# First MLP product turned token-major, two of its eight K pairs by a seven-product scheme, h kept in DRAM

## The chip, the cores and the metric

The kernel runs on one core of a Trainium2 chip. The metric is the device time of one execution in microseconds (us); the figure of a kernel is the median of several runs.

## The reference, cut to what matters

One layer of a hybrid block: 256 tokens, model width D = 2048, MLP width 8192, all in fp32. The part that the change touches is the end of it:

```
n = rms_norm(h);  h = h + concat(y_A, y_B) @ W_out          # mixers, out projection 2048 x 2048
h = h + square(relu(rms_norm(h) @ W1)) @ W2                  # W1 2048 x 8192, W2 8192 x 2048
out = rms_norm(h)
```

The row factor of the second `rms_norm` is taken out of the MLP: relu squared passes a positive row factor r on as r*r, and the kernel multiplies by it (`fs`) at the very end.

## The kernel before, in words

**How fp32 products are made.** TensorE multiplies in fp32r, a reduced fp32. So each operand is split into a rounded part hi and a remainder lo: ScalarE casts hi (`split`, L117) and VectorE subtracts lo = w - hi (L118). A product is the sum of three: hi*hi, hi*lo and lo*hi. A weight tile `w` of 128x2048 (1 MB) comes by one DMA of the SP queue into one of three buffers and is split in two pieces of 1024 columns. The split pairs have three buffers.

**Stages.** In projection and the two mixers (to 500 us of the span), out projection (L659, two halves `nh` of 1024 output columns, 508 to 555), first MLP product, here FF1 (L704 and L705, 555 to 919), second MLP product, here FF2 (L721, from 919), and the tail with the last norm.

**Out projection.** Each half accumulates four PSUM banks `accs`. VectorE adds each to the residual (L664) into `h`, which stays in SBUF to the end. ScalarE squares `h` for the norm (L666). TensorE transposes 128x128 blocks of `h` into the four banks `accb` (L673), and `to_T` writes them out, scaled by the norm's weight, as `hT`: ScalarE the hi part (L162), VectorE the lo part (L163). In `hT` each K block has 256 columns of hi and 256 of lo.

**FF1.** Output columns in 16 groups of four blocks of 128. The weight block is the stationary operand (128x128) and the activations move: L704 moves 512 columns (hi and lo of `hT` against hi of w) and L705 moves 256 (hi of `hT` against lo of w). The result stands feature-major, which is how FF2 wants its stationary operand. A group ends with four copies on ScalarE (L708) and on VectorE four additions (L709) and four relu-times-itself (L710), each 128x256, into `g`.

**FF2.** 64 K blocks `f`. `gs`, the split of a block of `g`, is stationary; the weights move in 512 columns; eight banks accumulate token-major.

**Pools and order.** PSUM has eight banks: pool `psA` (`acc`) has four, `psB` (`accb`) four. A scheduler in the framework sets one static order per engine from the program's text, and each engine carries out its own order, so an instruction that waits holds up all behind it on that engine.

Of the kernel before, what the change touches and what calls it, by code (L numbers as in the profile page):

```python
# [25 lines left out]
NM = NL + 1  # L26

_CONST_COLS = {}


def _constants():
# [42 lines left out]
def hybrid_block(ctx: ExitStack, tc: tile.TileContext, x, xt, w_in, w_ab, params, w_out, w_ff1, w_ff2,  # L74
# [14 lines left out]
    psA = ctx.enter_context(tc.tile_pool(name="psA", bufs=4, space=PSUM))  # L89

    yctx = ExitStack()
    ypool = yctx.enter_context(tc.tile_pool(name="ypool", bufs=1))
    NYA = 12
    yTa = ypool.tile([P, NYA, 2 * T], F32R, tag="yT", name="yTa")
# [7 lines left out]
    def acc_a():  # L102
        return psA.tile([P, 512], F32, tag="acc", name="acc")
# [19 lines left out]
        return hi, lo  # L123


    big = bpool.tile([P, 2 * D], F32, tag="h", name="big")
    x3 = big.rearrange("p (k t) -> p k t", k=KT)
    cst = cpool.tile([P, consts.shape[1]], F32, tag="cst", name="cst")
# [8 lines left out]
    SP.dma_start(cst, consts)  # L137
    wab = mp.tile([P, KT, 16], F32, tag="Xt", name="wab")
    SP.dma_start(wab, w_ab)

    def C(name):
        a, b = _CONST_COLS[name]
        return cst[:, a:b]

    ident, ones = C("ident"), C("ones")
    eps = C("eps")
# [14 lines left out]
    def to_T(dst, k, pt, wcol):  # L161
        ACT.activation(dst[:, k, 0:T], pt, AF.Copy, scale=wcol)  # L162
        DVE.scalar_tensor_tensor(out=dst[:, k, T:2 * T], in0=pt, scalar=wcol,  # L163
                                 in1=dst[:, k, 0:T].bitcast(F32), op0=ALU.mult, op1=ALU.subtract)
# [466 lines left out]
    mctx.close()  # L631


    psB = ctx.enter_context(tc.tile_pool(name="psB", bufs=4, space=PSUM))
# [5 lines left out]
    h = bpool.tile([P, 2 * D], F32, tag="h", name="h").rearrange("p (f c) -> p f c", f=2)  # L640
    for hf in range(2):
        SP.dma_start(h[:, hf, :], x[hf * P:(hf + 1) * P, :])
    octx = ExitStack()
    op = octx.enter_context(tc.tile_pool(name="op", bufs=1))
    sqj = op.tile([P, 1024], F32, tag="sqj", name="sqj")
    fs = cpool.tile([P, 16], F32, tag="fs", name="fs")
    for nh in range(2):
        accs = [acc_a() for _ in range(4)]
        for kp in range(8):
            w = wtile()  # L650
            SP.dma_start(w, w_out[nh * 8 + kp])
            for kk in range(2):
                k = 2 * kp + kk
                hi, lo = split(w[:, kk * 1024:(kk + 1) * 1024], 1024)
                for hf in range(2):
                    for a, ww in ((0, hi), (T, hi), (0, lo)):
                        st = yT(k, a + hf * P, a + hf * P + P)
                        for c in range(2):
                            PE.matmul(accs[2 * hf + c], lhsT=st, rhs=ww[:, c * 512:(c + 1) * 512],  # L659
                                      start=(k == 0 and a == 0 and ww is hi), stop=(k == 2 * NH - 1 and ww is lo))  # L660
        for hf in range(2):
            for c in range(2):
                hv = h[:, hf, nh * 1024 + c * 512:nh * 1024 + (c + 1) * 512]
                DVE.tensor_tensor(out=hv, in0=accs[2 * hf + c], in1=hv, op=ALU.add)  # L664
            hv = h[:, hf, nh * 1024:(nh + 1) * 1024]
            ACT.activation(sqj, hv, AF.Square, accum_out=fs[:, 2 * hf + nh:2 * hf + nh + 1])  # L666
        for k2 in range(4):
            pt = acc_b()
            for kk in range(2):
                k = nh * 8 + k2 * 2 + kk  # L670
                ptk = pt[:, kk * T:(kk + 1) * T]
                for hf in range(2):
                    PE.transpose(ptk[:, hf * P:(hf + 1) * P], h[:, hf, k * P:(k + 1) * P], ident)  # L673
                to_T(hT, k, ptk, cols[:, 16 + k:17 + k])
# [14 lines left out]
    def g(f):  # L689
        return gt[f // NG][:, f % NG, :]  # L690

    nfw = fp.tile([P, D], F32, tag="nfw", name="nfw")
    for fg in range(NF // 4):
        accs = [acc_a() if fg % 2 == 0 else acc_b() for _ in range(4)]
        for kq in range(4):
            w = wtile()
            SP.dma_start(w, w_ff1[fg * 4 + kq])
            for q in range(2):
                hi, lo = split(w[:, q * 1024:(q + 1) * 1024], 1024)
                for kk in range(2):  # L700
                    k = 4 * kq + 2 * q + kk
                    for f in range(4):
                        cs = slice(kk * 512 + f * P, kk * 512 + (f + 1) * P)
                        PE.matmul(accs[f], lhsT=hi[:, cs], rhs=hT[:, k, :], start=(k == 0), stop=False)  # L704
                        PE.matmul(accs[f][:, T:], lhsT=lo[:, cs], rhs=hT[:, k, 0:T], start=False, stop=(k == KT - 1))  # L705
        for f in range(4):
            lot = fp.tile([P, T], F32, tag="lotf", name="lotf", bufs=2)
            ACT.copy(lot, accs[f][:, T:])  # L708
            DVE.tensor_tensor(out=lot, in0=accs[f][:, 0:T], in1=lot, op=ALU.add)  # L709
            DVE.scalar_tensor_tensor(out=g(4 * fg + f), in0=lot, scalar=0.0, in1=lot, op0=ALU.max, op1=ALU.mult)  # L710
    SP.dma_start(nfw, norm_final_w.unsqueeze(0).to_broadcast([P, D]))

    accs = [[acc_a() for _ in range(4)], [acc_b() for _ in range(4)]]
    TAIL = 3
    held = []

    def ff2(f, hf, c, gs, hl):
        hi, lo = hl[c // 2]
        cs = slice((c % 2) * 512, (c % 2 + 1) * 512)
        for a, ww in ((0, hi), (T, hi), (0, lo)):  # L720
            PE.matmul(accs[hf][c], lhsT=gs[:, a + hf * P:a + hf * P + P], rhs=ww[:, cs],  # L721
                      start=(f == 0 and a == 0 and ww is hi), stop=(f == NF - 1 and ww is lo))

    keep = None
    for f in range(NF):
        w = wtile()
        SP.dma_start(w, w_ff2[f])
        gs = fp.tile([P, 2 * T], F32R, tag="gs", name="gs", bufs=4)
        split(g(f), None, gs[:, 0:T], gs[:, T:])
        n = f - (NF - TAIL)  # L730
        if n == 0:
            keep = fp.tile([P, TAIL - 1, 2, D], F32R, tag="g0", name="keep")
        hl = []
        for q in range(2):
            qs = slice(q * 1024, (q + 1) * 1024)
            if 0 <= n < TAIL - 1:
                hl.append(split(w[:, qs], None, keep[:, n, 0, qs], keep[:, n, 1, qs]))
            else:
                hl.append(split(w[:, qs], 1024))
        if n >= 0:  # L740
            held.append((f, gs, hl))
            continue
        for q in range(2):
            for hf in range(2):
                for c in (2 * q, 2 * q + 1):
                    ff2(f, hf, c, gs, hl)
    fin = fp.tile([P, 12], F32, tag="fin", name="fin")
    sqf = fp.tile([P, 512], F32, tag="sqf", name="sqf")
    o = fp.tile([P, D], F32, tag="o", name="o", bufs=1)
    NP = 5  # L750
    for hf in range(2):
        pieces = [(c * 512, (c + 1) * 512) for c in range(3)]
# [27 lines left out]
def _laid_out(i):  # L780

    import numpy as np

    w = i["w_in"][0]
    groups = []
    for base in (0, 4112):
        v = w[:, base:base + 4096].reshape(2, 8, P, 2, 2, NH, P)
        groups.append(v.transpose(5, 3, 0, 2, 1, 4, 6).reshape(4 * NH, P, 2048))

    def columns(a):  # L790
# [4 lines left out]
    return {  # L795
        "x": i["x"][0],
        "xt": i["x"][0].T.reshape(KT, P, T).transpose(1, 0, 2),
        "w_in": np.concatenate(groups),
        "w_ab": w[:, 4096:4112].reshape(KT, P, 16).transpose(1, 0, 2),
        "params": np.concatenate(params, 1),  # L800
        "w_out": i["w_out"][0].reshape(8, 2, P, 2, 1024).transpose(3, 0, 2, 1, 4).reshape(16, P, 2048),
        "w_ff1": i["w_ff1"][0].reshape(4, 4, P, 16, 512).transpose(3, 0, 2, 1, 4).reshape(64, P, 2048),
        "w_ff2": i["w_ff2"][0].reshape(64, P, 2048),
        "norm_final_w": i["norm_final_w"],
        "consts": _constants(),
    }
# [20 lines left out]
```

## Time and profile before

| | |
|---|---|
| median of 3 runs | 1275.83 us (1274.58 to 1276.43) |
| profiled execution, its own time | 1277.5 us |
| its span, first to last instruction | 1275.6 us |
| mean granted TensorE clock | 0.990 |
| busy: TensorE / VectorE / ScalarE / GpSimd | 97% / 67% / 53% / 14% |
| read from HBM | 225.83 MB |

A busy share is an average over all stages. Matmuls are pipelined, so the recorded length of one is longer than what it adds to the path: what it adds is read from the chain of the last-ending work, where so many matmuls stand against the time that they took together. PE is TensorE, DVE VectorE, ACT ScalarE, POOL GpSimd. A row such as "DVE lo L118 <- ACT hi L117" means that VectorE's subtraction waited for ScalarE's cast.

### The profile page before, as it was taken

To read this page: it belongs to the slowest core of one execution; us is meant where nothing else is said; L and a number is where in the kernel's file an instruction comes from. 1 tells how busy PE (TensorE), PEld (TensorE's weight loads), DVE (VectorE), ACT (ScalarE), POOL (GpSimd) and SP (SyncE) were. 2 spreads that over 40 slices of the span, in tenths; PEclk is the share of its full clock that TensorE was granted. 3 is DMA by queue.
4 is the path that set the end of the run, shared out by engine and by line. 5 is a ranking of instruction groups with operands and counts; after the bars stand their busy time and mean duration, and the time that the engine had idled before them with its cause. 6 is when DMAs were issued, how large, how long until landed. Compare 5 with 4: busy or idle time off the path is not lost.

```text
span 1275.6 us, 18490 instructions
## 1 busy us (share of the span) xinstructions
PE 1243.4 (97%) x7290; PEld 1054.2 (83%) x7290; DVE 857.5 (67%) x1200; ACT 674.2 (53%) x972; POOL 178.7 (14%) x224
## 2 busy tenths in 40 slices
PE   6999999998999999999999999999999999999997
PEld 5888888877788887888888888888888888888885
DVE  8789999889978996566555565555555555555556
ACT  7567677655667774555444444444444444444453
POOL 4233433278310130000000000000000000000000
PEclk9999999998999998999999999999999999999999
DMA  7445555543424544455555555555555555555552
GB/s 290 167 154 192 172 177 190 182 141 131 151 101 169 196 165 165 160 203 198 177 187 197 173 191 191 176 195 185 178 198 199 197 195 189 188 191 195 198 203 95
DMA packets 34646, 229.65 MB, mean 180 GB/s; under 512 B 4408, under 2 KB 5184, under 8 KB 7808
## 3 DMA queue, kind: packets, MB, share of 16 engines
q1 hardware_dynamic: 32256, 225.32, 50.1%
q0 software_dynamic: 1728, 2.11, 1.3%
q8 instruction: 57, 0.93, 0.3%
q10 hardware_dynamic: 576, 1.05, 0.2%
q14 instruction: 29, 0.24, 0.1%
HBM read 225.83 MB, written 2.63 MB: 179 GB/s over the span
## 4 chain that ended last, share of the span: by engine, by line
PE 91%; DVE 3%; POOL 3%; issue 2%; DMA 1%; ACT 0%; SPq 0%; POOLq 0%; DVEq 0%; ACTq 0%
PE acc L281 15%; PE acc L721 14%; PE accb L721 13%; PE accb L704 9%; PE acc L704 9%; PE acc L282 8%; PE acc L659 7%; PE accb L705 5%; PE acc L705 5%; POOL Xt L419 1%; POOL X L421 1%; DVE xT L163 1%; DMA big<-in_xt_dram 1%; PE pk L363 1%; DVE E L548 0%
## 5 line engine op out<-in xcount | busy, mean ns | idle before, releaser
L118 DVE TENSOR_TENSOR lo<-w,hi 128x1024 fp32r<-128x1024 f32 x408 | 511.9, 1256 | 362.9 <-ACT hi L117 362.3
L117 ACT CAST hi<-w 128x1024 fp32r<-128x1024 f32 (+1 forms) x416 | 432.7, 1042 | 442.4 <-PE accb L721 177.0
L281 PE MATMUL acc<-xT,hi 128*128 128x512 f32 x1024 | 363.7, 401 | 10.0 <-ACT hi L117 8.3
L282 PE MATMUL acc<-xT,lo 128*128 128x256 f32 x1024 | 283.6, 286 | 4.5 <-DVE lo L118 4.3
L281 PEld LDWEIGHTS acc<-xT,hi 128*128 128x128 f32 x1024 | 192.1, 191 | 50.1 <-ACT hi L117 8.3
L282 PEld LDWEIGHTS acc<-xT,lo 128*128 128x128 f32 x1024 | 195.7, 192 | 11.6 <-DVE lo L118 5.8
L704 PE MATMUL acc<-hT,hi 128*128 128x512 f32 x512 | 181.3, 399 | 0.0
L704 PE MATMUL accb<-hT,hi 128*128 128x512 f32 x512 | 180.8, 398 | 0.0
L721 PE MATMUL accb<-hi,gs 128*128 128x512 f32 x496 | 170.5, 389 | 0.0
L705 PE MATMUL accb<-hT,lo 128*128 128x256 f32 x512 | 143.2, 281 | 0.0
L705 PE MATMUL acc<-hT,lo 128*128 128x256 f32 x512 | 142.8, 281 | 0.0
L721 PE MATMUL acc<-hi,gs 128*128 128x512 f32 x496 | 133.4, 389 | 0.0
L704 PEld LDWEIGHTS accb<-hT,hi 128*128 128x128 f32 x512 | 96.1, 188 | 23.8
L704 PEld LDWEIGHTS acc<-hT,hi 128*128 128x128 f32 x512 | 96.1, 188 | 23.3
L159 POOL TENSOR_TENSOR fin<-fin,cst 128x1 f32<-128x1 f32 x2 | 1.1, 566 | 776.9 <-PE accb L721 769.5
L721 PEld LDWEIGHTS accb<-hi,gs 128*128 128x128 f32 x496 | 93.1, 188 | 19.4
L721 PEld LDWEIGHTS acc<-hi,gs 128*128 128x128 f32 x496 | 93.1, 188 | 19.2
L705 PEld LDWEIGHTS acc<-hT,lo 128*128 128x128 f32 x512 | 96.5, 189 | 0.2
L705 PEld LDWEIGHTS accb<-hT,lo 128*128 128x128 f32 x512 | 96.5, 189 | 0.1
L721 PE MATMUL accb<-lo,gs 128*128 128x512 f32 x248 | 95.8, 389 | 0.0
L721 PE MATMUL acc<-lo,gs 128*128 128x512 f32 x248 | 77.2, 389 | 0.0
L721 PEld LDWEIGHTS accb<-lo,gs 128*128 128x128 f32 x248 | 46.6, 188 | 9.7
(248 smaller groups left out, 1275.2 us busy)
## 6 DMA issues: line engine op xcount, KB each, us to landing
w<-in_w_ff_dram SPq DMA_DIRECT2D x128, 1024.0 KB, 4.9
w<-in_w_in_dram SPq DMA_DIRECT2D x62, 1024.0 KB, 5.0
w<-in_w_out_dram SPq DMA_DIRECT2D x16, 1024.0 KB, 4.9
big<-in_xt_dram SPq DMA_DIRECT2D x4, 512.0 KB, 7.7
w<-in_w_in_dram SPq DMA_DIRECT2D x4, 512.0 KB, 7.9
h<-in_x_dram SPq DMA_DIRECT2D x2, 1024.0 KB, 9.0
dt<-scr_g POOLq DMA_DIRECT2D x8, 128.0 KB, 5.6
nfw<-in_norm_final_w_dram SPq DMA_DIRECT2D x1, 1024.0 KB, 4.4
```

The costliest lines, as they stand in the source:

```text
L117: ACT.copy(hi, w)
L118: eng.tensor_tensor(out=lo, in0=w, in1=hi.bitcast(F32), op=ALU.subtract)
L163: DVE.scalar_tensor_tensor(out=dst[:, k, T:2 * T], in0=pt, scalar=wcol, in1=dst[:, k, 0:T].bitcast(F32), op0=ALU.mult, op1=ALU.subtract)
L281: PE.matmul(accs[g], lhsT=hi[:, kk, g, :], rhs=xT[:, k, :], start=(k == 0), stop=False)
L282: PE.matmul(accs[g][:, T:], lhsT=lo[:, kk, g, :], rhs=xT[:, k, 0:T], start=False, stop=(k == KT - 1))
L363: PE.matmul(pk0, lhsT=R[:, 1, 0:P], rhs=qk.rearrange("p a t -> p (a t)"), start=True, stop=True)
L419: POOL.tensor_tensor(out=t3, in0=X[:, j, j + 1:].unsqueeze(2).to_broadcast([np_, nr, ncol]), in1=X[:, j, 0:ncol].unsqueeze(1).to_broadcast ...
L421: POOL.tensor_tensor(out=X[:, j + 1:, 0:ncol], in0=X[:, j + 1:, 0:ncol], in1=t3, op=ALU.subtract)
L659: PE.matmul(accs[2 * hf + c], lhsT=st, rhs=ww[:, c * 512:(c + 1) * 512], start=(k == 0 and a == 0 and ww is hi), stop=(k == 2 * NH - 1 and ...
L704: PE.matmul(accs[f], lhsT=hi[:, cs], rhs=hT[:, k, :], start=(k == 0), stop=False)
L705: PE.matmul(accs[f][:, T:], lhsT=lo[:, cs], rhs=hT[:, k, 0:T], start=False, stop=(k == KT - 1))
L721: PE.matmul(accs[hf][c], lhsT=gs[:, a + hf * P:a + hf * P + P], rhs=ww[:, cs], start=(f == 0 and a == 0 and ww is hi), stop=(f == NF - 1 a ...
```

## The change

FF1 is written anew, and what it leans on around it is moved. Lines of the changed program stand in brackets below.

- **Turned round.** The activations are stationary (`sets`, `sets2`) and the weights move in 512 columns, so the result stands token-major. There are 8 groups `ng` of 1024 output columns (two halves of 512) and 8 K pairs `kp` of two K blocks. Two token halves, two K blocks, two column halves: eight 128x128x512 products for each K pair, each of three matmuls (`product`, L760 to L762).
- **Seven for eight.** For `SUMS = (0, 4)` seven products of sums stand for the eight. The sums of the activations are formed once (`X`, L703 to L710), those of the weights for each w tile on VectorE (`TT`, L793 with 1024 columns, L796 and L797 with 512), and the sums are split as other operands are. Seven banks p1 to p7 take the products, and four VectorE additions combine p1, p5, p6, p7 into `C4` (L811 to L814).
- **Plain pairs.** The other six K pairs accumulate onto p2, p3, p4 and an eighth bank p8. At a group's end VectorE adds the four banks onto `C4` (L835) and ScalarE takes the relu (L837).
- **Turned back.** FF2 wants the feature-major form: for each of the four pieces of `C4`, four TensorE transposes of 128x128 into p8 (L774) and one ScalarE square out of it into `g` (L775). These "fills" are called at fixed places in the next group; the last group's four fall into the first two K blocks of FF2.
- **Pools.** Eight banks `psF`, each with one buffer, are opened after `psA` and `psB` are closed. There are five split pairs instead of three (`hi2`, `lo2` are the added ones).
- **h.** Each half of `h` is written to DRAM after its additions (L687, four DMAs of 512 KB) and read back ahead of FF2 (L844, two of 1 MB) into `tail`, which takes the place of `sets`. The constants come in two DMAs in place of one.
- **FF2** has the same 1536 matmuls (L857 there). The product (hf 1, c 3) of its first two K blocks is done late, when p8 has been emptied.

The core of the diff:

```diff
-    hT = bpool.tile([P, KT, 2 * T], F32R, tag="xT", name="hT")
+    SUMS = (0, 4)
+    sets = bpool.tile([P, 8192], F32R, tag="xT", name="sets")
...
             ACT.activation(sqj, hv, AF.Square, accum_out=fs[:, 2 * hf + nh:2 * hf + nh + 1])
+            SP.dma_start(scr_h[hf, :, nh * 1024:(nh + 1) * 1024], hv)
...
+            X = op.tile([P, 8, P], F32, tag="X", name="X", bufs=2)
+            ACT.activation(view(X, P, [[-P, 2], [1, P]]), pt[:, 0:T].rearrange("p (a t) -> p a t", a=2), AF.Copy, scale=wc[0])
+            ACT.activation(X[:, 2:4, :].rearrange("p a t -> p (a t)"), pt[:, T:2 * T], AF.Copy, scale=wc[1])
+            DVE.tensor_tensor(out=X[:, 4], in0=X[:, 0], in1=X[:, 3], op=ALU.add)
+            DVE.tensor_tensor(out=X[:, 5], in0=X[:, 4], in1=X[:, 1], op=ALU.subtract)
+            POOL.tensor_tensor(out=X[:, 6], in0=X[:, 1], in1=X[:, 0], op=ALU.subtract)
+            DVE.tensor_tensor(out=X[:, 7], in0=X[:, 2], in1=X[:, 5], op=ALU.subtract)
+            st = a_sums(kp)
+            split(X[:, 1:8], None, st[:, 0], st[:, 1])
...
+    psF = ctx.enter_context(tc.tile_pool(name="psF", bufs=1, space=PSUM))
...
-                        PE.matmul(accs[f], lhsT=hi[:, cs], rhs=hT[:, k, :], start=(k == 0), stop=False)
-                        PE.matmul(accs[f][:, T:], lhsT=lo[:, cs], rhs=hT[:, k, 0:T], start=False, stop=(k == KT - 1))
...
+    def product(dst, a, b, start, stop):
+        (ah, al), (bh, bl) = a, b
+        PE.matmul(dst, lhsT=ah, rhs=bh, start=start, stop=False)
+        PE.matmul(dst, lhsT=al, rhs=bh, start=False, stop=False)
+        PE.matmul(dst, lhsT=ah, rhs=bl, start=False, stop=stop)
...
+        def go():
+            pt = bank(8)
+            for c in range(4):
+                PE.transpose(pt[:, c * P:(c + 1) * P], src[:, c * P:(c + 1) * P], ident)
+            ACT.activation(g(8 * ng + 4 * half, 4)[:, :, hf * P:(hf + 1) * P], pt.rearrange("p (c t) -> p c t", c=4),
+                           AF.Square)
...
+                B21, B22 = halves(split_pair(w[:, 1024:2048]))
+                DVE.tensor_tensor(out=TT[:, 0:1024].rearrange("p (a c) -> p a c", a=2), in0=view(w, 0, [[1536, 2], [1, 512]]),
+                                  in1=view(w, 512, [[-512, 2], [1, 512]]), op=ALU.subtract)
+                B1, B3 = halves(split_pair(TT[:, 0:1024]))
+                DVE.tensor_tensor(out=T2, in0=B[3], in1=T1, op=ALU.subtract)
+                DVE.tensor_tensor(out=T4, in0=B[2], in1=T2, op=ALU.subtract)
+                B2, B4 = halves(split_pair(TT[:, 1024:2048]))
...
+                for dst, a, b in ((p2, 1, B21), (p3, 6, B22), (p5, 3, B1), (p7, 5, B3), (p6, 4, B2), (p4, 2, B4),
+                                  (p1, 0, B11)):
+                    product(dst, A[a], b, kp == 0, kp == LAST_SUMS and a in (0, 3, 4, 5))
+                    if kp == 0 and a in (4, 0):
+                        fill()
...
+                for kk, b1, b2 in ((0, B11, B12), (1, B21, B22)):
+                    for dst, hf, b in ((p2, 0, b1), (p3, 0, b2), (p4, 1, b1)):
+                        product(dst, A(kk, hf), b, False, last and kk == 1)
+                        if kp == 1 and kk == 0:
+                            fill()
+                if first:
+                    p8 = bank(8)
+                for kk, b in ((0, B12), (1, B22)):
+                    product(p8, A(kk, 1), b, first and kk == 0, last and kk == 1)
...
+        for n, (at, p) in enumerate(((0, p2), (2, p3), (1, p4), (3, p8))):
+            DVE.tensor_tensor(out=C4[:, at], in0=p, in1=C4[:, at], op=ALU.add)
+        for n in range(4):
+            ACT.activation(C4[:, n], C4[:, n], AF.Relu)
+            fills.append(turn(ng, n, C4[:, n]))
```

**The hand-over to FF1 on TensorE, before.** `accb<-cst,h` are the transposes of `h`, `acc<-hT` the first matmuls of FF1.

```order
L659 MATMUL acc<-lo,yTb 128x512 x2
L673 MATMUL accb<-cst,h 128x128 x2
L704 MATMUL acc<-hT,hi 128x512
L705 MATMUL acc<-hT,lo 128x256
L704 MATMUL acc<-hT,hi 128x512
L705 MATMUL acc<-hT,lo 128x256
```

And now (the numbers behind a name tell buffers apart; the first `p` is p2). The row of the first FF1 matmul waits for VectorE's last L167, which is `to_T`'s lo part (L163 before) of the last transposed bank.

```order
L679 MATMUL acc<-lo,yTb 128x512 x2
L694 MATMUL accb<-cst,h 128x128 x16
L760 MATMUL p_5691<-hi,sets 128x512
L761 MATMUL p_5691<-hi,sets 128x512
L762 MATMUL p_5691<-lo,sets 128x512
L760 MATMUL p_5692<-hi,sets 128x512
```

The last 16 transposes stood in pairs between FF1's matmuls; now all of them stand ahead of FF1.

**A fill in the second group on TensorE, now.** `p_6077` and `p_6086` are both bank p8 as the third and the fourth fill use it, `p_6002` is p1, and `p_6104` is p8 again as an accumulator. The row of the fourth fill waits for ScalarE's square of the third, and the row behind it for the square of the fourth. Nothing like it stood there before.

```order
L760 MATMUL p_6002<-hi_6197,sets_5007 128x512
L774 MATMUL p_6077<-cst,C_5886 128x128 x4
L761 MATMUL p_6002<-hi_6197,sets_5007 128x512
L762 MATMUL p_6002<-lo_6198,sets_5007 128x512
L774 MATMUL p_6086<-cst,C_5886 128x128 x4
L760 MATMUL p_6104<-hi,sets 128x512
```

The products for p8 of the first three plain K blocks, put off until the fills are through, follow in one row: 15 matmuls.

**The end of a group on VectorE, before** (`lo<-w,hi` is the split, here in pieces of 1024 columns):

```order
L709 TENSOR_TENSOR lotf<-acc,lotf 128x256 x2
L710 SCALAR_TENSOR_TENSOR g_5652<-lotf 128x256 x2
L118 TENSOR_TENSOR lo<-w,hi 128x1024
L709 TENSOR_TENSOR lotf<-acc,lotf 128x256 x2
L710 SCALAR_TENSOR_TENSOR g_5652<-lotf 128x256 x2
L118 TENSOR_TENSOR lo<-w,hi 128x1024 x7
```

And now, at the end of the first group, from the sums of the next group's w tile on (`C_5886` is `C4`):

```order
L793 TENSOR_TENSOR TT<-w 128x1024
L120 TENSOR_TENSOR lo_6028<-w,hi_6027 128x512
L813 TENSOR_TENSOR C_5886<-p_5696,C_5886 128x512
L814 TENSOR_TENSOR C_5886<-p_5696,C_5886 128x512
L796 TENSOR_TENSOR TT<-w,TT 128x512
L120 TENSOR_TENSOR lo_5967<-w,hi_5966 128x1024
L120 TENSOR_TENSOR lo_6013<-w,hi_6012 128x1024
L797 TENSOR_TENSOR TT<-w,TT 128x512
L120 TENSOR_TENSOR lo<-TT,hi 128x1024 x2
L835 TENSOR_TENSOR C_5886<-p_5691,C_5886 128x512
```

The next group's sums and their splits stand ahead of the group's own evictions.

More of the change, by code (lines that the diff above doesn't have):

```diff
@@ L28 @@
 _CONST_COLS = {}
+NKEEP = 130
 def _constants():
@@ L123, in split @@
         return hi, lo
-    big = bpool.tile([P, 2 * D], F32, tag="h", name="big")
+    big = hpool.tile([P, 2 * D], F32, tag="h", name="big")
     x3 = big.rearrange("p (k t) -> p k t", k=KT)
-    cst = cpool.tile([P, consts.shape[1]], F32, tag="cst", name="cst")
+    cst = cpool.tile([P, NKEEP], F32, tag="cst", name="cst")
+    cst_a = mp.tile([P, consts.shape[1] - NKEEP], F32, tag="cst", name="cst_a")
     prm = cpool.tile([P, NPARAM], F32, tag="prm", name="prm")
@@ L673, in hybrid_block @@
                     PE.transpose(ptk[:, hf * P:(hf + 1) * P], h[:, hf, k * P:(k + 1) * P], ident)
-                to_T(hT, k, ptk, cols[:, 16 + k:17 + k])
+            kp = nh * 4 + k2
+            wc = [cols[:, 16 + 2 * kp + kk:17 + 2 * kp + kk] for kk in range(2)]
+            if kp in plain:
+                for kk in range(2):
+                    to_T(a_plain(kp), kk, pt[:, kk * T:(kk + 1) * T], wc[kk])
+                continue
+            X = op.tile([P, 8, P], F32, tag="X", name="X", bufs=2)
[7 more added lines that the diff above has]
+            split(X[:, 1:8], None, st[:, 0], st[:, 1])
     for hf in range(2):
@@ L687, in hybrid_block @@
     gt = [fp.tile([P, NG, T], F32, tag=f"g{i}", name=f"g{i}") for i in range(2)]
[L689 to L695, printed above, removed]
-            w = wtile()
[L697 to L710, printed above, removed]
@@ new lines, in g, with bank, pair, split_pair @@
+    def g(f, n=1):
+        return gt[f // NG][:, f % NG:f % NG + n, :]
+    def bank(i):
+        return psF.tile([P, 512], F32, tag=f"p{i}", name=f"p{i}")
+    pairs = [0]
+    def pair():
+        n = pairs[0] = pairs[0] + 1
+        pool, t = (spool, "") if n % 5 < 3 else (fp, "2")
+        return [pool.tile([P, 1024], F32R, tag=p + t, name=p + t, bufs=2 if t else 3) for p in ("hi", "lo")]
+    def split_pair(w):
+        hi, lo = pair()
+        split(w, None, hi, lo)
+        return hi, lo
@@ new lines, in hybrid_block, with fill @@
+    c1 = ExitStack()
+    cp = c1.enter_context(tc.tile_pool(name="cp", bufs=1))
+    t1 = ExitStack()
+    tp = t1.enter_context(tc.tile_pool(name="tp", bufs=1))
+    NGR = 8
+    KP = KT // 2
+    LAST_SUMS = SUMS[-1]
+    fills = []
+    def fill():
+        if fills:
+            fills.pop(0)()
+    def product(dst, a, b, start, stop):
[3 more added lines that the diff above has]
+        PE.matmul(dst, lhsT=ah, rhs=bl, start=False, stop=stop)
@@ new lines, in halves, with turn @@
+    def halves(hl):
+        return [[t[:, c * 512:(c + 1) * 512] for t in hl] for c in range(2)]
+    def turn(ng, n, src):
+        half, hf = n // 2, n % 2
+        def go():
[4 more added lines that the diff above has]
+                           AF.Square)
+        return go
@@ L711, in hybrid_block @@
+    t1.close()
+    f2 = ctx.enter_context(tc.tile_pool(name="f2", bufs=1, side="right"))
+    tail = bpool.tile([P, 8192], F32, tag="xT", name="tail")
+    h, nfw, o = tail[:, 0:2 * D].rearrange("p (f c) -> p f c", f=2), tail[:, 2 * D:3 * D], tail[:, 3 * D:]
+    for hf in range(2):
+        SP.dma_start(h[:, hf, :], scr_h[hf])
     SP.dma_start(nfw, norm_final_w.unsqueeze(0).to_broadcast([P, D]))
-    accs = [[acc_a() for _ in range(4)], [acc_b() for _ in range(4)]]
+    accs = [[None] * 4, [None] * 4]
@@ L714, in hybrid_block @@
+    for hf, c, i in ((0, 0, 1), (0, 1, 5), (1, 0, 6), (1, 1, 7), (0, 2, 2), (0, 3, 3), (1, 2, 4)):
+        accs[hf][c] = bank(i)
     TAIL = 3
@@ L724, in hybrid_block @@
     keep = None
+    late = []
     for f in range(NF):
@@ L738, in hybrid_block @@
             else:
-                hl.append(split(w[:, qs], 1024))
+                hl.append(split_pair(w[:, qs]))
         if n >= 0:
@@ L745, in hybrid_block @@
                 for c in (2 * q, 2 * q + 1):
[L746 to L749, printed above, removed]
+                    if f < 2 and (hf, c) == (1, 3):
+                        late.append((f, hf, c, gs, hl))
+                    else:
+                        ff2(f, hf, c, gs, hl)
+                    fill()
+        if f == 1:
+            accs[1][3] = bank(8)
+            for a in late:
+                ff2(*a)
+            c1.close()
+    fin = f2.tile([P, 12], F32, tag="fin", name="fin")
+    sqf = f2.tile([P, 512], F32, tag="sqf", name="sqf")
     NP = 5
@@ L801, in _laid_out @@
         "w_out": i["w_out"][0].reshape(8, 2, P, 2, 1024).transpose(3, 0, 2, 1, 4).reshape(16, P, 2048),
-        "w_ff1": i["w_ff1"][0].reshape(4, 4, P, 16, 512).transpose(3, 0, 2, 1, 4).reshape(64, P, 2048),
+        "w_ff1": np.concatenate([f1[:, kk, :, :, nb] for kk, nb in ((0, 1), (0, 0), (1, 0), (1, 1))], 3).transpose(2, 0, 1, 3)
+        .reshape(64, P, 2048),
         "w_ff2": i["w_ff2"][0].reshape(64, P, 2048),
```

58 lines of the change are left out of this document (50 added, 8 removed).

## The prediction

> **What bounds the kernel now.** I read the page's busy shares and its chain that ended last, then the chain and the waits inside FF1, then the windows of the hand-over.
>
> ```profile
> PE 1243.4 (97%) x7290; PEld 1054.2 (83%) x7290; DVE 857.5 (67%) x1200; ACT 674.2 (53%) x972; POOL 178.7 (14%) x224
> PE 91%; DVE 3%; POOL 3%; issue 2%; DMA 1%; ACT 0%; SPq 0%; POOLq 0%; DVEq 0%; ACTq 0%
> ...
> 570.00:918.00 348.00, 348.00 (x1974) 302.01 (x1973) 194.10 (x249) 150.00 (x189) 0.00 (x0) 1.00 0.53 187
> ```
>
> TensorE (PE) carries 91% of the chain. In FF1, 570 to 918, it has no gap at a granted clock of 1.00 (the column before the DMA share), while VectorE (DVE) is busy 194 of 348 us (56%), ScalarE (ACT) 43% and DMA 53%. Who waits there:
>
> ```profile
> DVE lo L118 <- ACT hi L117: 155.1, 123, 1.6
> ACT hi L117 <- PE accb L704: 95.0, 63, 1.8
> ACT hi L117 <- PE acc L704: 90.1, 60, 1.8
> ```
>
> The other engines wait for PE, and PE for none of them. So FF1 costs what its matmuls add to PE's path, and the change is priced on PE first, then by every wait that it puts in front of PE.
>
> ```profile
> 520.04 35.37 PE acc L659 x156
> 555.41 0.27 PE accb L673 x2
> ...
> 917.87 0.23 PE accb L704
> 918.10 0.12 PE accb L705
> 918.22 0.24 PE accb L704
> 918.46 0.12 PE accb L705
> 918.58 2.73 PE acc L721 x12
> ```
>
> The chain (start, length, count): a matmul that moves 512 columns adds 35.37/156 = 0.227 us in the out projection and 2.73/12 = 0.227 in FF2. FF1 runs from 555.4 to 918.6.
>
> **The change, part by part.**
>
> *1. FF1's matmuls.* Before: 363.1 us, less 16 transposes that stood in between (1.75, priced in part 2), is 361.4 for 1024 pairs of 512 and 256 columns, 0.353 a pair. (The rows above, 0.23 to 0.24 plus 0.12, agree.) After: a plain K pair has 8 products, a seven-product pair 7; so a group has 6x8 + 2x7 = 62 products, 186 matmuls, and eight groups 1488. Each loads a 128x128 stationary and moves 512 columns, the shape of FF2, so I take FF2's 0.227: 1488 x 0.2267 = 337.3 us. **-24.1 us.** Of this 48 matmuls that the scheme saves are 10.9; the other 13.2 come from moving 512 columns where a 256-column matmul stood (768 columns cost 0.353 before, 0.340 by FF2's rate). The bounds are nothing of these 13.2, or all.
>
> *2. Turning back.* 128 transposes (8 groups x 4 pieces x 4).
>
> ```profile
> 519.16 0.87 PE accb L673 x8
> L673 PE MATMUL accb<-cst,h 128*128 128x128 f32 x32 | 5.8, 283 | 0.0
> ```
>
> Eight in a row added 0.87 us, 0.109 each, though each is recorded as 283 ns long: records overlap. 128 x 0.109 = **+14.0 us**; by the pair at 555.41, 0.135 each, it is 17.3. The Trainium skill ("TensorE: Matmul & The Clock Gate", Part 4) gives about 275 ns for a transpose in a kernel's context; the trace agrees with that as the record's length, not as what it adds. Taken as the addition it would be an estimated 35 us, which the row of eight speaks against.
>
> *3. The hand-over to FF1.* Before, PE went from the last out-projection matmul (E, 555.4) straight on, with transposes strewn in. Now the first FF1 matmul waits for the last `to_T` of the last bank. I walk what stands between on ACT and DVE with these rows:
>
> ```profile
> 554.51 2.48 DVE L664 TENSOR_TENSOR h<-acc,h 128x512 f32<-128x512 f32 x4
> 555.00 1.05 ACT L117 CAST hi<-w 128x1024 fp32r<-128x1024 f32 x1 [1.67 <-PE acc L659]
> 555.96 1.05 ACT L666 ACTIVATE sqj<-h 128x1024 f32<-128x1024 f32 x1
> 556.90 1.22 DVE L118 TENSOR_TENSOR lo<-w,hi 128x1024 fp32r<-128x1024 f32 x1
> 556.91 0.18 ACT L666 ACTIVATION_READ_ACCUMULATOR sqj<-h 128x1 f32 x1
> 559.33 0.84 ACT L162 ACTIVATE hT<-accb,prm 128x256 fp32r<-128x256 f32 x2 [1.05 <-PE accb L673]
> 559.84 0.88 DVE L163 SCALAR_TENSOR_TENSOR hT<-accb,prm,hT 128x256 fp32r<-128x256 f32 x2 [0.96 <-ACT hT L162]
> ```
>
> DVE's four additions end at E+2 and the 16 transposes at about E+3. ACT from E: cast 1.05, square 1.25 with its read, two writes of `X` 0.85, square 1.25, three `to_T` 1.26, cast of the sums 0.92 (896 columns, from the 1.05 of 1024), three `to_T` 1.26, together 7.8. DVE gets the cast of the sums at E+6.6, subtracts for 1.1, then has three `to_T` of 0.44: E+9. So PE stands from E+3 to E+9. Against before, where the same transposes took 1.75, that is **+7.2 us** (bounds 4, if DVE and ACT run closer together, and 10). ACT's next cast also waits for the four writes of `h` to DRAM, and PE for that cast, twelve matmuls into FF1. The nearest rows are 512 KB in 7.7 us and 1 MB in 4.9: issued at E+1 and E+2.2 they land by E+10, and PE asks for the cast at E+12 or later. I take nothing; up to 3 us if they are late.
>
> ```profile
> big<-in_xt_dram SPq DMA_DIRECT2D x4, 512.0 KB, 7.7
> w<-in_w_ff_dram SPq DMA_DIRECT2D x128, 1024.0 KB, 4.9
> ...
> 500.00:504.00 4.00, 1.34 (x7) 0.94 (x5) 2.25 (x4) 2.02 (x4) 0.00 (x0) 0.92 0.30 115
> 504.00:507.00 3.00, 2.73 (x6) 2.15 (x7) 0.43 (x1) 0.22 (x1) 0.00 (x0) 0.50 0.87 322
> 507.00:510.00 3.00, 3.00 (x10) 2.31 (x9) 1.92 (x4) 1.05 (x2) 0.00 (x0) 0.50 0.05 19
> 510.00:515.00 5.00, 5.00 (x25) 4.14 (x25) 2.02 (x4) 2.93 (x6) 0.00 (x0) 0.98 0.01 3
> ...
> 503.82 0.41 ACT yTb L117
> 504.27 5.49 PE acc L659 x12
> 504.27 2.93 PE L659 MATMUL acc<-hi,yTb 128*128 128x512 f32 x6 [2.93 <-ACT yTb L117]
> 17.79 0.69 PE L281 MATMUL acc<-xT,hi 128*128 128x512 f32 x2 [1.73 <-DVE xT L163]
> 13.09 0.63 PE L281 MATMUL acc<-xT,hi 128*128 128x512 f32 x2
> ```
>
> *4. The clock after it.* PE idled 2.93 us before 504.27, and then ran at a clock of 0.50: twelve matmuls took 5.49 us, 0.457 each. Full speed was back at about 510, so half of 5.7 us was lost, 2.9. After a gap of 1.73 us at 17.79 two matmuls took 0.69 us, near the 0.63 of two at 13.09 without one. A gap of 6 us is past the first case: **+2.9 us** (nothing if the gap is under 2 us; 3.4 if it lasts longer). The Trainium skill (the same page, Part 1) has the clock at half after an idle window of about 3.4 us, and for about 3.4 us of busy time. The trace halves it after less and holds it longer; by the page this term would be an estimated 1.7.
>
> *5. The fills.* Of four in a group, the first two have other matmuls behind them. The fourth waits for ACT's square of the third with only two matmuls between, and the p8 matmuls wait for the square of the fourth with none.
>
> ```profile
> L763 ACT ACTIVATE sqf<-h 128x512 f32<-128x512 f32 x7 | 4.4, 630 | 10.5 <-DVE h L761 10.5
> L344 ACT ACTIVATE u<-pss,cst 128x512 f32<-128x512 f32 x8 | 5.6, 696 | 0.0
> ```
>
> A square out of PSUM takes 0.63 to 0.70, and a hand-over about 0.05 (ACT's yTb, 503.82 and 0.41 long, then PE at 504.27). First wait 0.72 - 0.45 = 0.27, second 0.72: 1.0 us, in groups two to eight, **+7.0 us**. If the second is partly covered it is 0.7 a group; if ACT is in a cast of 1.05 when the fill comes, 1.4: 4.9 to 9.8.
>
> *6. DVE in FF1.* It hides under PE, but with less room.
>
> ```profile
> L764 DVE TENSOR_TENSOR o<-h,nfw 128x512 f32<-128x512 f32 x7 | 4.8, 691 | 0.3
> L118 DVE TENSOR_TENSOR lo<-w,hi 128x1024 fp32r<-128x1024 f32 x124 | 152.0, 1225 | 155.1 <-ACT hi L117 155.1
> ```
>
> A group: plain pairs 6 x 2 x 1.23 = 14.8; two seven-product pairs, each 3 splits and one sum of 1024 (4.9) and a split and two sums of 512 (2.1), 13.9; eight additions 8 x 0.69 = 5.5. Together 34.2 us against PE's 186 x 0.227 + 1.7 + 1.0 = 44.9: 76%, from 56%. What goes (64 times L708 to L710) was hidden. The tight place is a group's end, where DVE has sums, splits and evictions of about 12 us in a row; five split pairs let it start early. I take nothing, and up to 1 us a group as a bound.
>
> *7. The rest.* h's 2 MB out and back, `tail` and the split constants are hidden: DMA is half idle, and reading `h` back has all of FF2 as cover. The first FF2 matmuls stand behind a cast that needs a pair back and behind the last fills: **+0.8** (0 to 2).
>
> **Sum:** -24.1 + 14.0 + 7.2 + 2.9 + 7.0 + 0.8 = **+7.8 us**. The profiled execution took 1277.5 us (span 1275.6), so its counterpart is 1285.3. The median of runs, 1275.8, is 1.7 lower; on it I forecast **1283.6 us**. With the low ends together (4, 0, 4.9, 0 for hand-over, clock, fills, FF2) the sum is -1.2, 1274.6; with the high ends (17.3, 13.4, 9.8, 2) it is +18.4, 1294.
>
> **Rivals.**
>
> *The hand-over is hidden (other side).* If PE's wait ahead of the first FF1 matmul stays so short that the clock holds, 10.1 us go: 1273.5, and with the fills at 0.7 a group 1271.4. It decides when the hand-over with its clock costs under 1.9 us at that fill price. For it: the additions at 554.51 began before E, and all data of the first K pairs are ready a half earlier. Against: PE's order puts the wait on the last `to_T`. Chance of ending faster this way 0.18.
>
> *Next to no change.* Hand-over and fills at their low ends, 1274.6: 0.08.
>
> *VectorE becomes the bound.* If the group's end makes PE wait 2.5 us in each of eight groups, for a split queued behind evictions that themselves wait for PE: +20, 1303. For it: 76% on average, and banks p1 to p8 without a second buffer. Against: 10 us of slack in a group. 0.12.
>
> *The turn brings no faster column.* If the new matmuls cost 0.353 for 768 columns, 1488 come to 350.2 us, 12.9 more: 1296.5. Against: FF2 is this shape and shows 0.227. 0.05.
>
> *The clock falls at each fill.* Seven times 2.9, 20 us: 1304. Against: two gaps of under 0.8 us, where 1.73 did no harm. 0.05.
>
> My forecast has 0.52, its own range 1277 to 1292. The range for 8 in 10 reaches down into the hidden hand-over and up past the third rival: 1270 to 1297. A measurement here can tell some 0.2% (2.5 us) from no change: faster 0.20, same 0.09, slower 0.71.
>
> **What would show it.** Right: FF1 with 1488 matmuls at 0.227 in the chain; one PE gap of about 6 us after the last out-projection matmul, released by DVE's last `to_T`, followed by a clock of 0.50 for some 6 us; in groups two to eight two short PE waits for ACT's square, about 1 us together; DVE about 76% busy. Wrong: no such gap or half clock (then 1271 to 1274); PE waiting for DVE's splits or sums at a group's start, by 2 us or more each time (then 1295 and up); or matmuls in FF1 at another pitch than FF2's.

## The result and the profile after

The changed kernel takes 1287.3 us, the median of four executions (1285.3 to 1288.8), against 1276.1 for the kernel before (1274.6 to 1277.5): 11.1 us slower, a ratio of 1.0088 (1.0073 to 1.0103). The forecast was 7.8 us slower.

The profiled execution took 1285.3 us, the lowest of the four, and its span is 1283.3, 7.7 above the span before. The page's busy line and its chain that ended last, by engine:

```profile
PE 1237.4 (96%) x6858; PEld 1029.3 (80%) x6858; DVE 916.0 (71%) x1220; ACT 713.6 (56%) x1014; POOL 179.8 (14%) x226
PE 90%; DVE 3%; POOL 3%; issue 2%; ACT 1%; DMA 1%; SPq 0%; POOLq 0%; DVEq 0%; ACTq 0%
```

And one window of FF1 (sum, then busy time of PE, PEld, DVE, ACT, POOL, then the granted clock):

```profile
570.00:918.00 348.00, 341.68 (x1542) 278.73 (x1541) 244.07 (x260) 182.81 (x220) 0.00 (x0) 1.00 0.52 186
```

TensorE is still the bound, but in FF1 it now has gaps: it is busy 341.7 us of 348, where it had no gap. VectorE rose to 244 of 348 us (70%; the forecast said about 76%). What PE waited for from the out projection on:

```profile
PE p L760 <- DVE sets L167: 5.7, 1, 5.7
PE p L760 <- ACT g L775: 4.8, 7, 0.7
PE acc L679 <- ACT yTb L119: 2.9, 1, 2.9
PE p L774 <- ACT g L775: 1.5, 7, 0.2
PE p L857 <- ACT hi L119: 0.5, 1, 0.5
```

The third row stood in the kernel before as well. The others are new: the hand-over to FF1 (5.7 us, once), the two waits of the fills (0.7 and 0.2 us, seven times each), and FF2's start (0.5). None is for a split or a sum of weights on VectorE.

The hand-over, from the timeline of PE, ACT and DVE (start, length; in brackets the idle time before it):

```profile
551.92 2.26 PE L694 MATMUL accb<-cst,h 128*128 128x128 f32 x16
552.62 1.05 ACT L686 ACTIVATE sqj<-h 128x1024 f32<-128x1024 f32 x1
554.38 1.05 ACT L686 ACTIVATE sqj<-h 128x1024 f32<-128x1024 f32 x1
556.49 0.95 ACT L119 CAST sets<-X 128x896 fp32r<-128x896 f32 x1
557.47 1.09 DVE L120 TENSOR_TENSOR sets<-X,sets 128x896 fp32r<-128x896 f32 x1 [0.19 <-ACT sets L119]
558.48 1.26 DVE L167 SCALAR_TENSOR_TENSOR sets<-accb,prm,sets 128x256 fp32r<-128x256 f32 x3
559.89 0.77 PE L760 MATMUL p<-hi,sets 128*128 128x512 f32 x1 [5.70 <-DVE sets L167]
```

It runs as the prediction walked it: squares, sums, cast, subtraction, the last three `to_T`, and then FF1's first matmul, 8.0 us after the first transpose. Windows for the clock, in the out projection and behind the hand-over:

```profile
504.00:507.00 3.00, 3.00 (x15) 2.43 (x15) 1.55 (x5) 0.70 (x1) 0.00 (x0) 1.00 0.77 311
560.00:564.00 4.00, 4.00 (x10) 3.15 (x11) 2.56 (x3) 1.63 (x2) 0.00 (x0) 0.52 0.26 53
564.00:568.00 4.00, 4.00 (x20) 3.28 (x19) 2.78 (x3) 2.73 (x3) 0.00 (x0) 1.00 0.69 236
```

The chain at one pair of fills (start, length):

```profile
893.91 0.23 PE p L760
894.14 0.45 PE p L774 x4
894.59 0.02 issue
894.61 0.61 ACT g L775
895.22 0.04 issue
895.26 0.67 PE p L774 x4
895.93 0.02 issue
895.95 0.61 ACT g L775
896.56 0.04 issue
896.60 0.50 PE p L760
897.10 0.23 PE p L761
```

After the hand-over PE ran four microseconds at half clock; behind that, over all of FF1, the clock was 1.00, at the fills too. In the out projection, where the same gap of 2.9 us had halved the clock in the profile before, this execution kept it at 1.00. At the fills PE stands while ACT takes each square, and the first work after each wait is slow: four transposes take 0.67 in place of 0.45, and a matmul 0.50 in place of 0.23.

### The profile page after: what moved, and what is told of

Its sections match the earlier page's. It is cut to its first block, busy times and chain, and to the rows that moved or that the text cites. A ratio compares the mean times of both kernels' runs of the same rounds, so it can differ in the third digit from the quotient of the medians.

```text
span 1283.3 us, 17709 instructions
## 1 busy us (share of the span) xinstructions
PE 1237.4 (96%) x6858; PEld 1029.3 (80%) x6858; DVE 916.0 (71%) x1220; ACT 713.6 (56%) x1014; POOL 179.8 (14%) x226
## 4 chain that ended last, share of the span: by engine, by line
PE 90%; DVE 3%; POOL 3%; issue 2%; ACT 1%; DMA 1%; SPq 0%; POOLq 0%; DVEq 0%; ACTq 0%
PE p L857 27%; PE acc L285 16%; PE p L760 9%; PE p L761 9%; PE p L762 9%; PE acc L286 8%; PE acc L679 7%; POOL Xt L423 1%; PE p L774 1%; POOL X L425 1%; ACT g L775 1%; DMA big<-in_xt_dram 1%; DVE xT L167 1%; PE pk L367 1%; DVE sums L177 0%
## 5 line engine op out<-in xcount | busy, mean ns | idle before, releaser
L120 DVE TENSOR_TENSOR lo<-w,hi 128x1024 fp32r<-128x1024 f32 (+1 forms) x408 | 497.7, 1231 | 284.7 <-ACT hi L119 283.8
L857 PE MATMUL p<-hi,gs 128*128 128x512 f32 x992 | 304.8, 389 | 0.5 <-ACT hi L119 0.5
L857 PEld LDWEIGHTS p<-hi,gs 128*128 128x128 f32 x992 | 186.0, 188 | 39.1 <-ACT hi L119 0.7
L760 PE MATMUL p<-hi,sets 128*128 128x512 f32 x496 | 196.2, 396 | 10.5 <-DVE sets L167 5.7
L761 PE MATMUL p<-hi,sets 128*128 128x512 f32 x496 | 193.8, 393 | 0.0
L857 PE MATMUL p<-lo,gs 128*128 128x512 f32 x496 | 192.1, 389 | 0.0
L762 PE MATMUL p<-lo,sets 128*128 128x512 f32 x496 | 182.8, 392 | 0.0
L760 PEld LDWEIGHTS p<-hi,sets 128*128 128x128 f32 x496 | 93.7, 189 | 32.1 <-ACT g L775 6.5
L762 PEld LDWEIGHTS p<-lo,sets 128*128 128x128 f32 x496 | 93.6, 189 | 19.4
L761 PEld LDWEIGHTS p<-hi,sets 128*128 128x128 f32 x496 | 93.6, 189 | 19.2
L857 PEld LDWEIGHTS p<-lo,gs 128*128 128x128 f32 x496 | 93.1, 188 | 19.4
L163 POOL TENSOR_TENSOR fin<-fin,cst 128x1 f32<-128x1 f32 x2 | 1.1, 563 | 721.3 <-DVE fin L162 721.3
L775 ACT ACTIVATE g<-p 128x512 f32<-128x512 f32 x32 | 19.1, 597 | 61.0 <-PE p L774 60.9
L679 PE MATMUL acc<-hi,yTa 128*128 128x512 f32 x192 | 52.6, 394 | 0.0
```

The lines of the kernel that those rows point to most:

```text
L120: eng.tensor_tensor(out=lo, in0=w, in1=hi.bitcast(F32), op=ALU.subtract)
L760: PE.matmul(dst, lhsT=ah, rhs=bh, start=start, stop=False)
L761: PE.matmul(dst, lhsT=al, rhs=bh, start=False, stop=False)
L762: PE.matmul(dst, lhsT=ah, rhs=bl, start=False, stop=stop)
L775: ACT.activation(g(8 * ng + 4 * half, 4)[:, :, hf * P:(hf + 1) * P], pt.rearrange("p (c t) -> p c t", c=4), AF.Square)
```

## The experiments

The times below are medians; the kernel before stood at 1276.2 to 1276.6 beside them. A step down is told against the changed kernel's 1287.3 or the experiment it is built on.

**No turning back** (e1). It leaves the transposes out, so FF2 works on other numbers. The code is shortened here, as in the cuts below.

```diff
-            pt = bank(8)
-            for c in range(4):
-                PE.transpose(pt[:, c * P:(c + 1) * P], src[:, c * P:(c + 1) * P], ident)
-            ACT.activation(g(...)[:, :, hf * P:(hf + 1) * P], pt.rearrange("p (c t) -> p c t", c=4), AF.Square)
+            ACT.activation(g(...)[:, :, hf * P:(hf + 1) * P], src.rearrange("p (c t) -> p c t", c=4), AF.Square)
```

> Left out: turning the MLP's activations back. ScalarE squares the token-major pieces straight from SBUF into g, without the 128 transposes and without a PSUM bank, so FF2 multiplies other numbers; all matmuls stay. Theory (transposes 14.0 us, and two PE waits for ScalarE's square at the fills of groups two to eight, 1.42 us each by the changed kernel's trace, 9.9 us): 24 us less than the changed kernel's 1287.3, about 1263. Rival (the waits at the fills only stand in for waits on VectorE's splits, which would come forward): 14 us less, about 1273.

1262.6 us, 24.7 less: the theory's number. Turning back costs 24 to 25 us, as much as all that the new matmuls save (24.1 by the forecast's sum). Nothing else came forward in its place: PE's waits in that run are the hand-over (5.7) and the gap in the out projection (2.9), no more.

**Own banks for the fills** (e4).

```diff
-            pt = bank(8)
+            pt = bank(8) if late else bank((5, 6, 7, 1)[n])
...
-                    if kp == 0 and a in (4, 0):
-                        fill()
...
-                        if kp == 1 and kk == 0:
-                            fill()
+                        if kp in (5, 6) and kk == 1 and dst is not p3:
+                            fill(False)
...
-                    C4 = cp.tile([P, 4, 512], F32, tag="C", name="C4")
+                    C4 = cp.tile([P, 4, 512], F32, tag="C", name="C4", bufs=2)
```

> The fills of groups two to eight go to K pairs five and six, where banks p5, p6, p7 and p1 rest, one bank for each fill; C4 has two buffers for it; p8 only accumulates. The last group's fills stay as they are. Theory (the fills' waits come from the one bank that transposes and accumulators share): PE waits for no square, 9 to 10 us less than the changed kernel's 1287.3, about 1277.5. Rival (the wait moves to VectorE's combination of p1, p5, p6, p7, which now has to come first): 0 to 4 us less, 1283 to 1287.

1277.6 us, 9.7 less: the theory's number again. PE's waits are now these three, and no row is left for ACT's square:

```profile
PE p L760 <- DVE sets L167: 5.7, 1, 5.7
PE acc L679 <- ACT yTb L119: 2.9, 1, 2.9
PE p L855 <- ACT hi L119: 0.5, 1, 0.5
```

So of the 24.7 us of turning back, some 15 are the transposes and FF2's start, and 10 come from the fills' waits. The waits name the bank: each was for ScalarE's square out of p8, which served the fills and an accumulator in turn. The edit also moves the fills and sets more matmuls between them; whether that alone would do, with p8 kept for all four, was not tried.

**Banks open across the hand-over** (e3).

```diff
-    psA = yctx.enter_context(tc.tile_pool(name="psA", bufs=4, space=PSUM))
+    psA = ctx.enter_context(tc.tile_pool(name="psA", bufs=1, space=PSUM))      # tags p1 to p4
...
-    psB = octx.enter_context(tc.tile_pool(name="psB", bufs=4, space=PSUM))
+    psB = ctx.enter_context(tc.tile_pool(name="psB", bufs=1, space=PSUM))      # tags p5 to p8
...
-        return psF.tile([P, 512], F32, tag=f"p{i}", name=f"p{i}")
+        return (psA if i < 5 else psB).tile([P, 512], F32, tag=f"p{i}", name=f"p{i}")
```

> The eight PSUM banks belong to pools that stay open from the out projection into FF1, each bank with a name of its own, so FF1's first matmuls wait for the readers of their own bank and not for the last reader of all. Theory (the 8 us gap ahead of FF1 and the half clock after it come from the pool's closing): gap under 2 us, clock 1.00 after it, 7 to 8 us less than the changed kernel's 1287.3, about 1279.5. Rival (the gap is the chain of activation sums, square and split, that FF1 needs anyway): 0 to 2 us less, 1285 to 1287.

1284.9 us, 2.4 less. The theory fell, and the rival's number holds nearly. PE does begin FF1 between the transposes, but after four products it stands again, and the clock falls all the same. The timeline of PE, and then a window:

```profile
557.95 0.40 PE L766 MATMUL p<-lo,sets 128*128 128x512 f32 x1
562.61 0.72 PE L764 MATMUL p<-hi,sets 128*128 128x512 f32 x1 [4.26 <-DVE sets L170]
```

```profile
564.00:568.00 4.00, 4.00 (x15) 3.22 (x14) 2.72 (x4) 2.09 (x3) 0.00 (x0) 0.74 0.36 88
```

The pool's closing was only the first of two waits on the same chain: K pair 0 wants banks p5 to p7, and these are free only when the sums and `to_T` have read them.

**Both** (e5).

> Open banks and own banks for the fills together. Theory (two separate losses): their sum, 17 to 18 us less than the changed kernel's 1287.3, about 1269.5, faster than the kernel before by 6. Rival (with PE freed of these waits VectorE, 76% busy, becomes the bound): half of the sum or less, 1278 or more.

1275.5 us, 11.8 less, which is about e3's 2.4 and e4's 9.7 together: two separate losses, as the theory had it. Its number, 17 to 18, was missed, since e3 gave 2.4 where I had taken 7 to 8. VectorE did not become the bound: no wait of PE for its splits or sums shows in FF1's groups. The ratio to the kernel before is 0.9990 (0.9981 to 0.9999), inside the 0.2% that counts as no change here.

**Without the scheme** (e6, on e5): `SUMS = ()`, no `X`, no `TT`, and VectorE takes the relu straight out of PSUM.

> Built on e5_both, without the seven-product scheme: all eight K pairs plain, 1536 matmuls in FF1 in place of 1488, no sums on VectorE, no C4 combination, relu on VectorE out of PSUM. Theory (the scheme saves its 48 matmuls on PE's path, and its sums lie beside PE): 10.9 us more for the matmuls, 2 to 3 less because the sums of activations are gone from the hand-over, 0.9 less because no matmul reads its weights from sets2 (0.233 us each there, 0.227 elsewhere in the changed kernel's trace): 6 to 8 us above e5_both's 1275.5, about 1282.5. Rival (VectorE's load takes back what the scheme saves): within 2 us of 1275.5.

1280.9 us, 5.4 more than e5; its ratio to the kernel before is 1.0033 (1.0020 to 1.0045). The theory holds, a little below its range, and the trace says why: the hand-over lost more than I had allowed. PE's gaps there are 0.9 and 0.6 us at full clock. e5 had a gap of 4.3 us, and half clock behind it, which cost 2.9 us in its own trace and 1.7 in e3's; I take 2. So 10.9 for the 48 matmuls, less 4.8 for the hand-over, less 0.9 for `sets2`, is 5.2.

**Squares later in the text** (e7, on e5): ScalarE's squares written behind the transposes.

> Built on e5_both; ScalarE's four squares of h for the norm come after the activations have been written, since the norm's factor is wanted only at the end. With open banks PE still stood 4.3 us, behind the to_T of its fourth bank, after four products. Theory (that gap is ScalarE's chain, two squares of 1.25 us ahead in it): 2.5 us less, about 1273; with the gap then near 2 us perhaps also the clock, 1271. Rival (VectorE's part of the chain is as long): 0 to 1 us less, 1274.5 to 1275.5.

1275.4 us. It says nothing of either: the scheduler put the squares where they had stood, ahead of `X`, and the gap is the same 4.26 us.

**Plain K pairs first** (e8, on e7).

```diff
-        for kp in range(KP):
+        for kp in (1, 2, 0, 3, 4, 5, 6, 7) if ng == 0 else range(KP):
```

> Built on e7_late_squares; the first group takes K pairs 1 and 2 ahead of 0, whose products need only banks that are free early (p2, p3, p4), so PE has some 8 us of matmuls while ScalarE and VectorE finish the last banks. Theory (the gap and the half clock are all that is left of the hand-over): both go, 4.3 + 2 us less than e5_both's 1275.5, about 1269. Rival (the same chain then stands ahead of p8, or casts of w behind it in ScalarE's order starve PE): no better than e7_late_squares, 1273.

1273.7 us, 1.8 less than e5. This lies between theory and rival: the clock stayed at 1.00 in the profiled execution, but two gaps are left. The timeline of PE, and then two windows:

```profile
554.95 0.44 PE L698 MATMUL p<-cst,h 128*128 128x128 f32 x2 [0.97 <-DVE h L689]
564.32 0.48 PE L767 MATMUL p<-hi,sets 128*128 128x512 f32 x1 [2.41 <-DVE sets L170]
```

```profile
560.00:564.00 4.00, 1.90 (x11) 1.30 (x9) 4.00 (x13) 2.99 (x7) 0.04 (x1) 1.00 0.80 273
564.00:568.00 4.00, 3.69 (x16) 3.11 (x17) 3.28 (x5) 4.00 (x5) 0.00 (x0) 1.00 0.00 0
```

VectorE is busy for all of the first 4 us (the third pair of columns), and PE waits for its last `to_T`. The gap of 0.97 us is new: VectorE's order now has a sum of weights for K pair 0 ahead of the out projection's additions, which the transposes wait for:

```profile
553.08 1.22 DVE L800 TENSOR_TENSOR TT<-w 128x1024 f32<-128x1024 f32 x1
554.21 1.28 DVE L689 TENSOR_TENSOR h<-p,h 128x512 f32<-128x512 f32 x2
```

**Squares out of the hand-over** (e9, on e8): they are taken from `tail` at FF2's start.

> Built on e8_plain_first; the four squares of h are taken from the copy that is read back at FF2's start, so ScalarE has none of them at the hand-over (in e7_late_squares the scheduler had put them where they stood, and that run told nothing of them). e8_plain_first had PE waits of 1.0 and 2.4 us left there at full clock. Theory (ScalarE's squares, 2.5 us in front of to_T, are the last of the gap): 2 to 2.5 us less than e8_plain_first's 1273.7, about 1271.5. Rival (VectorE's own additions, sums and to_T, busy without a break there, are the chain): under 1 us less.

1273.6 us, no change, and the gap is 2.38. The rival holds: ScalarE had room, and VectorE's additions, sums and `to_T` are the chain. In this profiled execution half clock followed the gap, where in e8's it had not:

```profile
564.00:568.00 4.00, 4.00 (x12) 3.09 (x12) 3.69 (x4) 3.65 (x5) 0.00 (x0) 0.61 0.19 27
```

**Sums early** (e10, on e9): `SUMS = (0, 2)`, the first group in the order 1, 3, 0, 2, 4 and so on.

> Built on e9_tail_squares; the seven-product pairs are K pairs 0 and 2 in place of 0 and 4, both of the first half of the out projection, so no sums of activations are formed at the hand-over, and the first group runs K pairs 1 and 3 first. Theory (the sums, cast and subtraction there, 0.9 us more on ScalarE and 1 us more on VectorE than two plain banks' to_T): 0 to 1.5 us less than e9_tail_squares. Beside it: the matmuls of K pair 4, whose weights lay in the tile sets2, took 0.233 us each in the changed kernel; if it is the tile, K pair 2 now shows 0.233, if it is what runs beside K pair 4, K pair 2 shows 0.227.

1271.1 us, 2.5 less than e9, more than the theory had: the 2.4 us gap is gone whole, and with it the half clock that could follow it. PE's waits are these:

```profile
PE p L683 <- ACT yTb L122: 2.9, 1, 2.9
PE p L697 <- DVE h L688: 1.0, 1, 1.0
PE p L862 <- ACT hi L122: 0.5, 1, 0.5
PE p L759 <- DVE lo L123: 0.2, 1, 0.2
```

This version beats both kernels: its ratio to the kernel before is 0.9958 (0.9947 to 0.9970), 5.4 us less.

**A third K pair** (e11, on e10): `SUMS = (0, 1, 2)`, a `sets2` of twice the size, and K pair 3 first.

> Built on e10_early_sums; K pair 1 takes the seven-product scheme too (pairs 0, 1 and 2 of eight), sets2 holds two of the three sets of sums, and the first group begins with K pair 3. Theory (PE still bounds FF1): 24 matmuls fewer, 5.4 us, less 1.0 for 168 more matmuls with weights out of sets2 at 0.233: 4 to 5 us less than e10_early_sums's 1271.1, about 1266.7. Rival (VectorE becomes the bound: a group's 34.2 us grow by 4.5 to 38.7 of PE's 43, 90%): PE waits for sums and splits at a group's start, 1271 or more.

1274.1 us, 3.0 more than e10. It has the rival's sign and a part of its reason. VectorE is not full: it is busy 284 of 348 us. PE's waits in FF1 are five, for casts of weights and of their sums, in the first group alone. The waits, and then two windows, of FF1 and of the stretch behind the longest wait:

```profile
PE p L757 <- ACT hi L122: 4.3, 5, 2.8
```

```profile
570.00:918.00 348.00, 344.58 (x1547) 281.31 (x1548) 283.52 (x309) 200.92 (x244) 0.00 (x0) 0.99 0.54 195
578.00:585.00 7.00, 6.51 (x16) 4.21 (x15) 5.12 (x5) 3.35 (x4) 0.00 (x0) 0.53 0.56 170
```

The timeline of PE and ACT shows what the casts are:

```profile
568.86 1.05 ACT L122 CAST hi<-TT 128x1024 fp32r<-128x1024 f32 x1 [3.06 <-DVE TT L790]
575.59 1.04 ACT L122 CAST hi<-w 128x1024 fp32r<-128x1024 f32 x1 [1.91 <-DMA w<-in_w_ff_dram]
576.54 1.04 ACT L122 CAST hi<-TT 128x1024 fp32r<-128x1024 f32 x1
577.63 0.50 PE L757 MATMUL p<-hi,sets 128*128 128x512 f32 x1 [2.75 <-ACT hi L122]
```

Four of the five waits end with a cast of sums (`hi<-TT`). Some of these casts had waited for VectorE's sum (first row); the one of the longest wait stood behind a cast of weights that had waited 1.91 us for its DMA. Half clock from 578 to 585 cost about 3 us more in this execution. With the 4.3 us of waits that is about the 7.4 us by which the theory's 1266.7 was missed. Why those weights came late stays open.

With one plain pair to begin with, the first group asks for sums and splits sooner than they are made. Whether the scheme would pay for a third pair with the first group left plain was not tried.

## Why the prediction was right, and where it was off

The kernel came out 11.1 us slower where 7.8 were forecast, at 1287.3 us, inside the forecast's own range of 1277 to 1292. The mechanism held term by term: the time that a matmul adds, the transposes, the one wait at the hand-over with half clock behind it, and the two waits at the fills. The sizes were less good, and their errors cancel in part: the hand-over and the clock were taken 1 us too high each, the matmuls and the fills too low, by 1.9 and 2.9.

**Matmuls (-24.1).** Right in kind. The chain in FF2 and, in FF1, starts 0.227 apart show the pitch that was taken. Between FF1's first matmul (559.89) and FF2's first, in the chain, lie 363.7 us:

```profile
923.59 5.22 PE p L857 x23
```

337.3 of it are 1488 matmuls at 0.2267. The rival that the turn brings no faster column falls with it. A small part was missed; the timeline of PE:

```profile
901.95 1.07 PE L762 MATMUL p<-lo,sets 128*128 128x512 f32 x4
902.86 0.40 PE L760 MATMUL p<-hi,sets 128*128 128x512 f32 x1
906.12 0.63 PE L762 MATMUL p<-lo,sets 128*128 128x512 f32 x2
```

The four matmuls from 901.95 took 0.91 us, 0.228 each; the fourteen from 902.86 on, of K pair 4, whose weights lie in `sets2`, took 3.26, 0.233 each. Over K pair 4 that is 0.9 us, and about 1.0 is spread over the rest.

**Transposes (+14.0).** Right: a lone fill lengthens the path by 0.44 us, four times 0.11, and e4's time less e1's leaves 15.0 for the transposes with FF2's start.

**Hand-over (+7.2) and clock (+2.9).** The chain was the one that was walked. It took 8.0 us for 9.0, so +6.2, and PE ran at half clock for 3.9 us after it, not the 5.7 that I took, so about +1.9: the half clock had begun inside the gap (0.50 from 557 to 560). The rival that the hand-over is hidden rested on the first K pairs' data being ready a half earlier; e3 and e8 show that this helps only as far as banks are free. The writes of `h` to DRAM held up no work of PE; they landed in 2.7 us.

```profile
scr_h<-h SPq DMA_DIRECT2D x4, 512.0 KB, 2.7
```

**Fills (+7.0).** This term was mis-sized. From 894.14 to 897.10 are 2.96 us; eight transposes and three matmuls without a wait are 0.87 + 0.68. So 1.41 us are lost at each pair of fills, 9.9 in seven groups. I counted the waits (4.8 + 1.5 = 6.3 in the table) and left out the slow restart behind each: 0.22 for the transposes and 0.27 for the matmul. e4 measured 9.7. The clock did not fall at the fills, so that rival is out.

**VectorE (0) and FF2's start (+0.8).** Right. No wait of PE for VectorE's splits or sums shows in FF1, so the rival that VectorE becomes the bound is out for this kernel. At FF2's start a wait of 0.5 us shows.

The terms as the trace has them: -24.1 + 0.9 + 1.0 + 14.0 + 6.2 + 1.9 + 9.9 + 0.8 = +10.6, beside 11.1 by the medians. The profiled pair shows only 7.7 because this execution reached the end of the out projection at 551.9, where the one before had 555.4: of these 3.5 us, some 2.9 are the clock that did not fall at 504. That my sum came out at the profiled pair's number is chance.

## What to carry to other kernels

A product that is turned round for a better matmul shape must be turned back, and the price is not the transposes alone: give each turn a PSUM bank that rests at that time, or every hand-over to another engine costs the wait and a slow restart besides. Where a stage ends, list what the next stage's first instructions need, banks as well as data; opening one barrier shows only the next one. Here it took four steps (own banks, open banks, plain pairs first, sums early) until a part of the saved matmuls reached the time: 5.4 us of 24.1, of which the transposes keep some 14. Price a saving of matmuls against the engine that prepares the next stage's operands at the hand-over, not against its share over the stage.

## What was not expected of the hardware

The same gap keeps or halves the clock from one profiled execution to the next. After the 2.9 us gap in the out projection, which all these kernels have, the granted clock at 504 to 507 was 0.50 in the profile before, 1.00 in the changed kernel's, and 0.59 and 1.00 in e8's and e10's. After the 2.4 us gap at the hand-over it was 1.00 in e8's and 0.61 in e9's. In the profile before, some 6 us at half clock cost 3 us. The kernel before scatters over 4.5 us (1274.2 to 1278.7 over all its executions); that this gap is behind a part of that is likely, but not shown, since each kernel was profiled once. The Trainium skill ("TensorE: Matmul & The Clock Gate", Part 1) says that the activity window is free-running, so that the point of change varies. The traces agree with that. The same part has the clock at half after an idle window of about 3.4 us; the traces do not agree with that length, since 2.9 and once 2.4 were enough.

Matmuls with weights out of `sets2` took 0.233 us and those out of `sets` 0.227. In e10 the tile belongs to K pair 2, and the longer pitch went with it: 0.233 in runs of 24 or 25 matmuls, one run in a group. In e11 it holds K pairs 1 and 2, and in most groups the runs are 46 to 49 long, while K pair 0, a pair of sums too but out of `sets`, kept 0.227. So the pitch goes with the tile, and not with K pair 4 or with the last pair of sums. What it is about the tile stays open.
